# Twelve row gathers a layer move from the value blocks to the key blocks of a PEER layer

## The chip, the cores and the metric

The kernel runs on one core of a Trainium2 chip, which holds five engines that run side by side: TensorE (PE, with its weight loads as PEld), VectorE (DVE), ScalarE (ACT), GpSimd (POOL) and SyncE (SP, which here only issues transfers). The metric is the device time of one execution in microseconds.

## The reference

A trunk of two layers over 512 positions of width 1024. Each layer has a mixer (a spatial gating group and a stick-breaking attention group, which the change does not touch) and a retrieval layer, PEER, which takes most of the time. Cut to PEER:

```python
def peer_ffn(h, wq, k1, k2, u_tab, v_tab):      # 8 heads, 128 keys a half, 16384 experts
    ...
        q = (xb @ wq).reshape(PEER_BLOCK, PEER_HEADS, 2, PEER_HALF)
        ...                                     # top 16 of each half, top 16 of their sums
        eid = jnp.take_along_axis(cand_id, top_pos, axis=-1)
        g = jax.nn.softmax(top_s, axis=-1)
        ue = u_tab[eid]
        ve = v_tab[eid]
        act = jax.nn.gelu(jnp.einsum('pd,phkd->phk', xb, ue))
        return jnp.einsum('phk,phkd->pd', g.astype(xb.dtype) * act, ve)
```

So each position picks 8 x 16 = 128 experts; an expert has one key row `u` and one value row `v` of 1024 numbers.

## The kernel before

The 512 positions are four tiles of 128. They are treated in two ways. For three tiles (384 positions) the kernel is dense: it multiplies all 16384 experts, in 128 blocks of 128 experts, and weighs each product by how much the position wants that expert. For the fourth tile it gathers: for each of its 128 choices one indirect transfer brings 128 rows of 4 KB (512 KB) from the table of keys, and later one from the table of values, 256 gathers a layer.

Dense work. A key block (`u_item`, lines 128 to 130 through `mm3`) is 24 matmuls of 384 columns into a PSUM tile `u`, from one 512 KB weight tile `raw`; ACT splits the weights into `hi` (line 114) and DVE into `lo` (line 117), so that three products make one of full precision. ACT then writes gelu of the result to `act` (line 539, or line 536 into `gu`, where DVE multiplies it into `act` in line 537). A value block (`v_item`) is 18 matmuls of 512 columns into six PSUM tiles `acc`, from one 512 KB tile `wide` or `raw`; beside `hi` and `lo` of the weights it needs `hh` (ACT, line 114) and `hl` (DVE, line 117) of that block's `act`. How much each position wants each expert is made by one-hot products: DVE builds one-hots for 16 positions at once (lines 758, 761 and 765), PE multiplies them for 8 positions at a time (`spread`, lines 773 and 774) into a PSUM tile, and `weigh` brings that to `act` (DVE line 788, ACT line 790). In the second half of the keys that tile is the other one of the two `u` tiles, so it must be emptied before the next key block but one uses it.

Gathered work. Each gather is issued by POOL (line 822) into one of three buffers `grow_`. DVE then multiplies the rows: the first 128 with the activations, to 128 dots (line 825); after the last of them gelu and the weights; the other 128 with these weights, summed up in `hrow` (lines 831 and 833). These are called the gather's product below.

Order. In this part the program's order is written out by hand: each engine runs its instructions in the order in which they were written. `PLAN` has four stages: key blocks 32 to 63, value blocks of the first half, key blocks 64 to 127, value blocks 64 to 127. Each line of it has the kind, the blocks, whether one-hot products are made there (48 of them, spread over the stage) and a number of gathers, which are spread evenly over the blocks:

```python
n1 = min(gathers, (i + 1) * gathers // (n - (6 if bs[-1] == last else 0)))
```

`last` is 127, so that both of the last two stages leave the gathers out of their last 6 blocks. The last stage takes what is left of the 256. What a block brings beside its matmuls is written in the middle of it, in this order (`meanwhile`):

```python
fresh = [spread(*hot.pop(0)) for _ in range(steps[i][1])]
while late:
    late.pop(0)()                  # the products of line 537
for part in fresh:
    weigh(*part)
...                                # hh and hl of the next value block; one-hots
due = min(steps[i][2], len(left))
if due:
    gather(left.pop(0))
prepare(i + LOOK)                  # weights of the block after next: hi and lo
for _ in range(due - 1):
    gather(left.pop(0))
```

So the first gather of a block stands ahead of `lo` for the block after next on DVE, and a second gather behind it. A block with two gathers is called doubled.

Of the kernel before, what the change touches and what calls it, by code (L numbers as in the profile page):

```python
# [31 lines left out]
NK = 128  # L32
# [5 lines left out]
CH = NK // 2  # L38
NS2 = 11
NS1 = CH - NS2  # L40
# [18 lines left out]
FIRST = 2 * UNIT  # L59
HEAD = 1  # L60
MID = 2
PLAN = [("u", range(FIRST, CH), 1, 2),
        ("v", [*range(NS1, CH), *range(NS1)], 0, 100),
        ("u", range(CH, NK), 1, 64),
        ("v", range(CH, NK), 0, 2 * P)]


# [1 line left out]
def trunk(ctx: ExitStack, tc: tile.TileContext, x, rows1, rows2, ada, w_qk, w_row, w_o, wq, kt, wst,  # L69
# [423 lines left out]
    def peer(l):  # L493
        with tc.tile_pool(name="pe", bufs=1) as pe, \
# [237 lines left out]
            with tc.tile_pool(name="gp", bufs=1) as gp, ExitStack() as psc:  # L732
# [61 lines left out]

                order_v = [*PLAN[1][1], *PLAN[3][1]]

# [86 lines left out]

                first, last = PLAN[1][1][0], PLAN[3][1][-1]
                manual = ExitStack()
                manual.enter_context(tc.manual_schedule())
                final, steps, row = [], [], []
                chunk = -1
                for side, bs, spreads, gathers in PLAN:
                    items = [(u_item if side == "u" else v_item)(b) for b in bs]  # L890
# [91 lines left out]
```

## Time and profile before

| what | before |
|---|---|
| median of 3 runs | 3149.47 us (3141.75 to 3155.02) |
| the profiled execution | 3151.26 us, span 3149.6 us |
| PE busy | 2988.5 us, 95% of the span |
| DVE busy | 2485.8 us, 79% |
| POOL busy | 798.6 us, 25% |
| mean rate of all transfers | 207 GB/s |

Times in the profile count from the start of the span. The profiled execution's own time is 1.8 us above the median of the runs. In layer 0 the four stages begin at 573.79, 733.47, 1010.09 and 1317.87 us, in layer 1 at 2119.60, 2279.28, 2553.93 and 2858.00 us; the 58 gathering blocks of the last stage end at 1576.72 and 3110.07 us.

### The profile page before, as it was taken

What the parts mean: (1) busy time and instruction counts of PE and PEld (TensorE: products, weight loads), DVE (VectorE), ACT (ScalarE), POOL (GpSimd) and SP (SyncE); (2) the same over time, 40 slices, a digit from 0 to 9 for tenths busy, and PEclk for the clock granted to TensorE, in tenths of its full rate; (3) what the DMA queues carried; (4) which work ended last, traced back from release to release, by engine and by line L of the source; (5) the groups of instructions that cost most, each with busy time, mean ns of one, the idle gap of its engine ahead of it and who ended that gap; (6) DMA issues with size and microseconds to landing.
All of it is one profiled execution on the core that took longest, in us unless ns stands there. A gap on an engine that the chain in (4) does not pass through costs nothing. (4 is left out here: it accounts for less than half of the span.)

```text
span 3149.6 us, 47135 instructions
## 1 busy us (share of the span) xinstructions
PE 2988.5 (95%) x17532; PEld 2612.1 (83%) x17532; DVE 2485.8 (79%) x4951; ACT 1167.8 (37%) x2016; POOL 798.6 (25%) x584
## 2 busy tenths in 40 slices
PE   5988999999999999999999999999999999999998
PEld 4777888998777999977778888889987789998776
DVE  7687798797778889777853558969887888997787
ACT  3263333333333433333343633324333334333332
POOL 0000000003545323244500000000055543333452
PEclk8999999999999999999999999999999999999999
DMA  8746233337888666688832032333388876667885
GB/s 301 253 159 208 88 101 113 109 108 257 304 305 283 248 215 238 228 313 302 287 117 94 3 107 90 105 114 114 129 307 307 306 268 235 227 233 271 320 304 202
DMA packets 178840, 651.45 MB, mean 207 GB/s; under 512 B 19850, under 2 KB 20274, under 8 KB 178610
## 3 DMA queue, kind: packets, MB, share of 16 engines
q1 hardware_dynamic: 104018, 378.14, 35.8%
q0 software_dynamic: 73728, 268.47, 22.7%
q8 instruction: 137, 2.24, 0.3%
q10 hardware_dynamic: 864, 1.84, 0.2%
q14 instruction: 93, 0.76, 0.1%
HBM read 642.08 MB, written 6.29 MB: 206 GB/s over the span
## 5 line engine op out<-in xcount | busy, mean ns | idle before, releaser
L128 PE MATMUL u<-hh,hi 128*128 128x384 f32 x1920 | 665.1, 346 | 20.1 <-ACT act L539 17.3
L130 PE MATMUL u<-hh,lo 128*128 128x384 f32 x1920 | 648.2, 338 | 5.5 <-DVE lo L117 5.5
L129 PE MATMUL u<-hl,hi 128*128 128x384 f32 x1920 | 647.2, 337 | 0.0
L130 PE MATMUL acc<-hi,hl 128*128 128x512 f32 x1536 | 607.8, 396 | 32.8 <-DVE hl L117 32.5
L129 PE MATMUL acc<-lo,hh 128*128 128x512 f32 x1536 | 602.8, 392 | 7.0 <-DVE lo L117 6.9
L128 PE MATMUL acc<-hi,hh 128*128 128x512 f32 x1536 | 601.1, 391 | 0.0
L117 DVE TENSOR_TENSOR lo<-raw,hi 128x1024 fp32r<-128x1024 f32 x350 | 426.6, 1221 | 193.3 <-ACT hi L114 192.5
L114 ACT ACTIVATE hi<-raw 128x1024 fp32r<-128x1024 f32 x352 | 372.5, 1059 | 521.4 <-PE b L129 132.1
L114 ACT ACTIVATE hh<-act 128x384 fp32r<-128x384 f32 x256 | 134.4, 525 | 680.6 <-PE acc L129 677.5
L128 PEld LDWEIGHTS u<-hh,hi 128*128 128x128 f32 x1920 | 363.9, 190 | 24.7 <-ACT act L539 18.6
L130 PEld LDWEIGHTS acc<-hi,hl 128*128 128x128 f32 x1536 | 289.5, 188 | 113.3 <-DVE hl L117 54.3
L130 PEld LDWEIGHTS u<-hh,lo 128*128 128x128 f32 x1920 | 363.5, 189 | 6.6 <-DVE lo L117 6.6
L129 PEld LDWEIGHTS u<-hl,hi 128*128 128x128 f32 x1920 | 364.4, 190 | 1.4
L129 PEld LDWEIGHTS acc<-lo,hh 128*128 128x128 f32 x1536 | 289.7, 189 | 75.3 <-DVE lo L117 15.1
L128 PEld LDWEIGHTS acc<-hi,hh 128*128 128x128 f32 x1536 | 289.9, 189 | 57.9
L117 DVE TENSOR_TENSOR lo<-wide,hi 128x1024 fp32r<-128x1024 f32 x232 | 283.0, 1220 | 2.2 <-ACT hi L114 2.2
L114 ACT ACTIVATE hi<-wide 128x1024 fp32r<-128x1024 f32 x232 | 242.7, 1046 | 0.0
L117 DVE TENSOR_TENSOR hl<-act,hh 128x384 fp32r<-128x384 f32 (+1 forms) x272 | 152.8, 562 | 17.6 <-ACT hh L114 16.3
L128 PE MATMUL b<-hh,hi 128*128 128x512 f32 x336 | 132.5, 395 | 21.0 <-DVE hh L116 21.0
L234 DVE SCALAR_TENSOR_TENSOR aw<-aw,crow 128x1024 f32<-128x1024 f32 x96 | 116.9, 1222 | 44.9 <-DMA aw<-in_ada 44.6
L536 ACT ACTIVATE gu<-u 128x384 f32<-128x384 f32 (+23 forms) x186 | 63.7, 343 | 199.0 <-PE u L130 199.0
L129 PE MATMUL b<-hl,hi 128*128 128x512 f32 x336 | 131.1, 392 | 0.5 <-DVE hl L117 0.5
(1519 smaller groups left out, 5071.2 us busy)
## 6 DMA issues: line engine op xcount, KB each, us to landing
raw<-in_ut SPq DMA_DIRECT2D x240, 512.0 KB, 3.5
wide<-in_v_rows SPq DMA_DIRECT2D x232, 512.0 KB, 5.0
aw<-in_ada SPq DMA_DIRECT2D x96, 512.0 KB, 4.3
raw<-in_wq SPq DMA_DIRECT2D x32, 512.0 KB, 3.4
raw<-in_w_row SPq DMA_DIRECT2D x24, 512.0 KB, 4.2
raw<-in_v_rows SPq DMA_DIRECT2D x24, 512.0 KB, 6.0
raw<-in_w_qk SPq DMA_DIRECT2D x16, 512.0 KB, 3.5
raw<-in_w_o SPq DMA_DIRECT2D x16, 512.0 KB, 4.0
```

The source lines that it names most:

```text
L114: A.activation(dst_hi, src, AF.Copy)
L117: sub.tensor_tensor(dst_lo, src, dst_hi.bitcast(F32), OP.subtract)
L128: T.matmul(o, lh, rh, start=first, stop=False)
L129: T.matmul(o, lh, rl, start=False, stop=False)
L130: T.matmul(o, ll, rh, start=False, stop=last)
L234: V.scalar_tensor_tensor(aw, aw, 1.0, crow[0], op0=OP.mult, op1=OP.mult, accum_out=modc[:, l, j:j + 1])
L536: A.activation(g[:, :n], pu[:, :n], AF.Gelu_apprx_tanh)
```

## The change

The numbers of gathers in `PLAN` change. The first key stage gets 4 in place of 2, the first value stage 94 for 100, the second key stage 74 for 64, and the last value stage the rest, 84 for 90. In both layers.

```diff
-PLAN = [("u", range(FIRST, CH), 1, 2),
-        ("v", [*range(NS1, CH), *range(NS1)], 0, 100),
-        ("u", range(CH, NK), 1, 64),
+PLAN = [("u", range(FIRST, CH), 1, 4),
+        ("v", [*range(NS1, CH), *range(NS1)], 0, 94),
+        ("u", range(CH, NK), 1, 74),
         ("v", range(CH, NK), 0, 2 * P)]
```

With it the doubled blocks of the second key stage, counted from 0, go from 9, 19, 28, 38, 48 and 57 to 3, 7, 10, 14, 18, 21, 25, 28, 32, 36, 39, 43, 47, 50, 54 and 57; the blocks 3, 10, 18, 25, 28, 43 and 50 also build one-hots (before, 28, 38 and 48). The doubled blocks of the value stages become fewer: 94 gathers over 64 blocks for 100, and 84 over 58 for 90.

In a value stage this is what DVE finds in its order. Before, from block 7 of the first value stage of layer 0 on (`lo` is for weights, `hl` for the next block's `act`, the rows of line 825 are gathers' products):

```order
L825 SCALAR_TENSOR_TENSOR grow__7176,dots<-grow__7176,hrow 128x1024
L117 TENSOR_TENSOR lo<-wide,hi 128x1024
L825 SCALAR_TENSOR_TENSOR grow__7185,dots<-grow__7185,hrow 128x1024
L117 TENSOR_TENSOR hl<-act_2506,hh 128x3x128
L825 SCALAR_TENSOR_TENSOR grow__7208,dots<-grow__7208,hrow 128x1024
L117 TENSOR_TENSOR lo<-wide,hi 128x1024
L825 SCALAR_TENSOR_TENSOR grow__7217,dots<-grow__7217,hrow 128x1024
L117 TENSOR_TENSOR hl<-act_2506,hh 128x3x128
```

And with the change, from the same block on:

```order
L825 SCALAR_TENSOR_TENSOR grow__7182,dots<-grow__7182,hrow 128x1024
L117 TENSOR_TENSOR lo<-wide,hi 128x1024
L117 TENSOR_TENSOR hl<-act_2506,hh 128x3x128
L825 SCALAR_TENSOR_TENSOR grow__7211,dots<-grow__7211,hrow 128x1024
L117 TENSOR_TENSOR lo<-wide,hi 128x1024
L825 SCALAR_TENSOR_TENSOR grow__7220,dots<-grow__7220,hrow 128x1024
L117 TENSOR_TENSOR hl<-act_2506,hh 128x3x128
```

Block 7 has lost its second product, which stood ahead of the next block's `hl`; block 8 is as it was.

In the second key stage the same table adds products to DVE. Before, block 43 of layer 0 (one-hots, one product, `lo`, then the updates of `act` of block 44):

```order
L758 TENSOR_TENSOR wide<-iot,i2t 128x2048
L761 TENSOR_TENSOR om<-iot,i1t 128x1024
L765 TENSOR_TENSOR wide<-om,gt 128x1024 x2
L833 SCALAR_TENSOR_TENSOR hrow<-grow__11386,gg,hrow 128x1024
L117 TENSOR_TENSOR lo<-raw,hi 128x1024
L537 TENSOR_TENSOR act<-act,gu 128x272
L788 SCALAR_TENSOR_TENSOR act_2506<-u_11423,act_2506 128x11x8
L788 SCALAR_TENSOR_TENSOR act<-u_11423,act 128x33x8
```

And with the change:

```order
L758 TENSOR_TENSOR wide<-iot,i2t 128x2048
L761 TENSOR_TENSOR om<-iot,i1t 128x1024
L765 TENSOR_TENSOR wide<-om,gt 128x1024 x2
L833 SCALAR_TENSOR_TENSOR hrow<-grow__11395,gg,hrow 128x1024
L117 TENSOR_TENSOR lo<-raw,hi 128x1024
L833 SCALAR_TENSOR_TENSOR hrow<-grow__11404,gg,hrow 128x1024
L537 TENSOR_TENSOR act<-act,gu 128x272
L788 SCALAR_TENSOR_TENSOR act_2506<-u_11435,act_2506 128x11x8
L788 SCALAR_TENSOR_TENSOR act<-u_11435,act 128x33x8
```

A second product has come between `lo` and the updates that empty the PSUM tile of block 44's one-hot products.

## Rows read from the trace of the kernel before

**Rows 1.** The page's first part: busy time, share of the span and number of instructions of each engine.

```profile
PE 2988.5 (95%) x17532; PEld 2612.1 (83%) x17532; DVE 2485.8 (79%) x4951; ACT 1167.8 (37%) x2016; POOL 798.6 (25%) x584
```

**Rows 2.** Busy time by stretch: start and end of the stretch, its length, then busy time and number of instructions of PE, PEld, DVE, ACT and POOL, the granted share of TensorE's clock, the busy share of the DMA engines and GB/s. In order: layer 0's first key stage, the first 16 and the other 48 blocks of its first value stage, its second key stage, the 58 gathering blocks of its second value stage; layer 1's first value stage in the same two parts.

```profile
573.79:733.47 159.68, 159.68 (x1537) 155.29 (x1537) 143.30 (x221) 63.45 (x174) 5.39 (x4) 1.00 0.37 123
733.47:798.79 65.32, 65.32 (x289) 54.10 (x289) 52.00 (x76) 24.07 (x34) 33.66 (x23) 1.00 0.85 297
798.79:1010.09 211.30, 202.12 (x866) 160.91 (x865) 166.50 (x247) 69.88 (x95) 107.64 (x76) 1.00 0.85 301
1010.09:1317.87 307.78, 298.67 (x2305) 289.04 (x2304) 266.18 (x408) 116.52 (x244) 98.42 (x68) 0.99 0.64 231
1317.87:1576.72 258.85, 244.80 (x1046) 196.03 (x1045) 202.97 (x205) 86.07 (x118) 126.47 (x87) 0.99 0.84 297
2279.28:2344.60 65.32, 65.32 (x289) 54.10 (x289) 52.97 (x78) 24.05 (x34) 34.72 (x24) 1.00 0.86 303
2344.60:2553.93 209.33, 200.72 (x865) 161.06 (x864) 167.36 (x246) 69.61 (x94) 106.73 (x75) 1.00 0.86 303
```

**Rows 3.** PE's waits in the other 48 blocks of layer 0's first value stage (798.79 to 1010.09): who waited for whom, us in total, times, longest.

```profile
PE acc L130 <- DVE hl L117: 6.6, 9, 1.2
PE acc L129 <- DVE lo L117: 2.4, 5, 0.7
```

**Rows 4.** Single instructions in the second value stage of layer 0, in order of time: start, length, engine, line, operation, what it writes and reads; in brackets the engine's idle time before it and what ended it.

```profile
1531.10 1.28 DVE L833 SCALAR_TENSOR_TENSOR hrow<-grow__13927,gg,hrow 128x1024 f32<-128x1024 f32 x1 [0.89 <-DMA grow__13927<-in_v_rows,ids]
...
1532.65 1.68 POOL L822 DMA_INDIRECT grow__13968<-in_v_rows,ids  x1 [2.10 <-DVE hrow L833]
...
1536.68 1.22 DVE L117 TENSOR_TENSOR lo<-wide,hi 128x1024 fp32r<-128x1024 f32 x1
...
1540.96 1.28 DVE L833 SCALAR_TENSOR_TENSOR hrow<-grow__13968,gg,hrow 128x1024 f32<-128x1024 f32 x1 [3.06 <-DMA grow__13968<-in_v_rows,ids]
...
1542.77 0.50 PE L130 MATMUL acc<-hi,hl 128*128 128x512 f32 x1 [3.11 <-DVE hl L117]
```

**Rows 5.** Busy time by stretch, as in rows 2, ahead of that wait's end and after it.

```profile
1538.00:1542.00 4.00, 1.65 (x8) 1.03 (x6) 1.04 (x1) 1.47 (x2) 0.71 (x1) 1.00 0.92 324
1542.00:1547.00 5.00, 4.23 (x12) 3.33 (x13) 5.00 (x7) 0.00 (x0) 2.71 (x3) 0.66 0.57 162
```

**Rows 6.** Six gathers issued one after the other in the same stage; the last number is the time from issue to landing in us.

```profile
grow__13837<-in_v_rows,ids POOLq DMA_INDIRECT x1, 5.6
grow__13866<-in_v_rows,ids POOLq DMA_INDIRECT x1, 6.5
grow__13875<-in_v_rows,ids POOLq DMA_INDIRECT x1, 5.4
grow__13898<-in_v_rows,ids POOLq DMA_INDIRECT x1, 7.9
grow__13927<-in_v_rows,ids POOLq DMA_INDIRECT x1, 7.9
grow__13936<-in_v_rows,ids POOLq DMA_INDIRECT x1, 6.9
```

**Rows 7.** Busy time by stretch of line 833 alone, the gathers' products in the second value stages of layers 0 and 1: the stretch and its length, busy time and number on DVE, granted clock, DMA share, GB/s.

```profile
1317.87:1576.72 258.85, 113.46 (x89) 0.99 0.84 297
2858.00:3110.07 252.07, 112.99 (x89) 0.99 0.85 304
```

**Rows 8.** Single instructions at blocks 48 and 49 of layer 0's second key stage, as in rows 4.

```profile
1248.17 1.28 DVE L833 SCALAR_TENSOR_TENSOR hrow<-grow__11670,gg,hrow 128x1024 f32<-128x1024 f32 x1
...
1250.51 1.28 DVE L833 SCALAR_TENSOR_TENSOR hrow<-grow__11679,gg,hrow 128x1024 f32<-128x1024 f32 x1
...
1252.09 0.62 DVE L788 SCALAR_TENSOR_TENSOR act<-u,act 128x88 f32<-128x88 f32 x2
...
1252.80 0.27 ACT L790 ACTIVATE act<-u 128x120 f32<-128x120 f32 x1 [4.42 <-DVE act L788]
...
1253.13 0.44 PE L128 MATMUL u<-hh,hi 128*128 128x384 f32 x1 [0.64 <-ACT act L790]
```

**Rows 9.** PE's waits in layer 0's second key stage (1010.09 to 1317.87), as in rows 3.

```profile
PE u L773 <- ACT act L539: 4.2, 4, 2.2
PE u L130 <- DVE lo L117: 3.4, 2, 2.0
PE u L128 <- ACT act L790: 1.3, 3, 0.6
```

**Rows 10.** Busy time by stretch, as in rows 2, for groups of five blocks of layer 0's second key stage: blocks 16 to 20, and then every group from 26 to 30 up to 51 to 55.

```profile
1088.85:1111.99 23.14, 23.14 (x185) 22.51 (x185) 20.32 (x38) 9.53 (x19) 7.85 (x6) 1.00 0.61 226
...
1139.07:1163.04 23.97, 23.69 (x186) 22.67 (x185) 21.78 (x32) 9.03 (x19) 7.84 (x6) 1.00 0.61 219
1163.04:1186.19 23.15, 23.15 (x186) 22.52 (x186) 21.39 (x33) 9.13 (x19) 6.90 (x5) 1.00 0.68 241
1186.19:1210.29 24.10, 23.57 (x185) 22.56 (x185) 22.44 (x32) 8.88 (x19) 8.89 (x6) 1.00 0.64 230
1210.29:1233.92 23.63, 23.32 (x185) 22.62 (x185) 21.92 (x32) 8.73 (x19) 8.21 (x5) 1.00 0.63 228
1233.92:1258.22 24.30, 23.60 (x185) 22.57 (x185) 23.11 (x33) 8.61 (x19) 9.82 (x6) 1.00 0.65 232
1258.22:1282.24 24.02, 23.32 (x185) 22.62 (x185) 22.45 (x32) 8.35 (x19) 8.08 (x5) 1.00 0.63 226
```

## The prediction, made before the changed kernel ran

> **What bounds the kernel now.** I read the page's first part, then a table of busy time by stage, then the waits of TensorE in each stage, then single instructions where the longest waits stand. The page says that PE is busy 95% of the span [rows 1], so what a change can win is the time in which PE waits, and the table by stage says where that is [rows 2]. In the first key stage of layer 0 (573.79 to 733.47) PE is busy for all of its 159.68 us. In the first value stage it is busy for all of the first 16 blocks (65.32 us, 4.0825 us a block), and for only 202.12 of the 211.30 us of the other 48. The second key stage loses 9 of 307.78 us and the second value stage 14 of 258.85. (Busy time hides part of a stall, since a matmul's end is modelled; block times show all of it.)
>
> A value block that waits for nothing takes 4.0825 us. So the value stages hold these stalls: first stage, layer 0: 65.32 + 211.30 - 64 x 4.0825 = 15.3 us; layer 1: 65.32 + 209.33 - 261.3 = 13.4 us; second stage, the 58 blocks that gather: 258.85 - 58 x 4.0825 = 22.1 us in layer 0 and, with the time of [rows 7], 252.07 - 236.8 = 15.3 us in layer 1. Together 66 us, the most that the value blocks can give.
>
> Why they wait: PE's waits there all end with DVE's `hl` or `lo` [rows 3], and DVE was late because it stood at a gather's product. The longest case shows the chain [rows 4]: DVE finishes `lo` at 1537.9, its next instruction is the product of grow__13968, whose gather has not landed; DVE idles 3.06 us, does the product at 1540.96, then `hl`, and PE has waited 3.11 us for that `hl`. The clock granted to TensorE is 0.66 of full speed over the next 5 us, where it was 1.00 before [rows 5], so such a wait costs more than itself.
>
> Why the gather is late: it was issued at 1532.65, and POOL had waited for the product of grow__13927 (1531.10 to 1532.38), which frees the buffer; there are three buffers. So gathers run in a circle: product 1.28 us, about 0.27 us to the issue, landing 5.4 to 7.9 us after it, mean 6.7 over six in a row [rows 6]. That is 8.25 us for three gathers, 2.75 each, before any wait behind `lo` and `hl` in DVE's order. The second value stage of layer 0 did 89 products in 258.85 us [rows 7], 2.91 us each, and 89 in 252.07 us in layer 1, 2.83. PE alone would take 4.0825 us x 58 blocks / 90 gathers = 2.63 us a gather: the gathers, not PE, set the pace there. The first 16 blocks are free of stalls since three gathers lie ready and DVE starts ahead.
>
> The DMA rule of the Trainium skill would have it otherwise. Its page "DMA: Bandwidth & Descriptors", section "Anatomy of one DMA — SWDGE (gpsimd) path", gives 2.0 us plus the bytes at 436 GB/s, an estimate of 3.2 us for these 512 KB. By that the circle would be 4.8 us, 1.6 us a gather, far below PE's need, and nothing would be won. The rows say 5.4 to 7.9 us beside the weight stream, so here the trace disagrees, and the rows decide.
>
> **The change, part by part.** Value blocks, 6 gathers fewer in each stage. If gathers set the pace, a stage's time follows their number until PE's own time is reached. First stage: 276.62 x 94/100 = 260.0 us and 274.65 x 0.94 = 258.2 us, both just below PE's 261.3: no stall by the mean (PE's own time per gather rises from 2.61 to 2.78 us). Second: 258.85 x 84/90 = 241.6, 4.8 us above 236.8; 252.07 x 84/90 = 235.3, below it. But landings are uneven, and pace and need are now nearly equal, so single late landings still reach PE. I keep a fifth of today's stall for that: 3.1 and 2.7 us in the first stages, 3.1 us in the second stage of layer 1, and the 4.8 us of layer 0. So 66 us become 13.7, and 52 us are won. The bounds: all 66, if the head start of the first 16 blocks covers the unevenness; a half, 33, if single late landings weigh more than the mean.
>
> First key stage, 2 more gathers (blocks 7 and 23 beside 15 and 31). Each adds one product to DVE, whose busy time is 143.30 of 159.68 us, and PE waits for nothing there [rows 2]; the two gathers that it has today cost PE nothing. Cost 0; if that cover of 16 us were used up, 2 x 1.28 = 2.6 us a layer.
>
> Second key stage, 10 more gathers. Spread over 58 blocks, two products now fall into one block 16 times instead of 6. The circle does not press here: the three buffers serve 1.28 gathers per 4.7 us, 3.7 us each, against the 2.75 to 2.91 that they can do. The price is DVE's time. An extra product stands ahead of the block's `act` updates, which empty the PSUM tile that the next key block needs. The row for one such block late in the stage shows it [rows 8]: two products at 1248.17 and 1250.51, the update at 1252.09, ACT's part at 1252.80 after 4.42 us of idling, and PE waits 0.64 us for that. PE's waits in the stage are of this sort [rows 9], beside two at its start and one at the end of the first 128 gathers, which stay.
>
> To price it I cut the stage into groups of five blocks, which repeat [rows 10]. A group without a stall takes 23.15 us (1163.04). An early group with a doubled block (1088.85) takes 23.14: no cost, DVE has 2.8 us to spare. Three late ones with a doubled block that also builds one-hots take 23.97, 24.10 and 24.30, and the groups behind the last two 23.63 and 24.02. So the three cost 0.82, 0.95 + 0.48 and 1.15 + 0.87: 1.4 us each on average, the dearest 2.0. Of the ten added, about half come in the first 25 blocks; there DVE still has some 2.8 us a group, and I put 0.3 us on each for the denser rhythm. The others meet a DVE that is busy 21.4 to 23.1 of 23.15 us, and I put their own 1.28 us on each, near the mean measured. That is 1.5 + 6.4 = 7.9 us a layer, 16 us in all. The bounds: nothing, as the early pair shows, and 2.0 us for each of ten in both layers, 40 us; I take the value nearest the late rows for the late half alone.
>
> Traffic only moves: DMA's share is 0.64 in this key stage against 0.85 in the value stages, so ten more transfers of 512 KB fit. POOL is busy 98 of 307.78 us. The products change place, not number.
>
> Sum: -52 + 16 = -36 us. The profiled execution took 3151.3 us, so 3115; the median of the three runs is 1.8 us lower, so **3113 us**.
>
> **Rivals.** *The stall stays.* Each of PE's waits follows one late landing, and landings might be as late with fewer gathers, since the weight stream beside them is the same. Then the value blocks give nothing and the key blocks cost 16 us: 3165 us, or 3182 with the dearest price on the late half and 1.28 us on the early one. It ends slower once less than 16 of the 66 us go. Against it: the first 16 blocks have the same weight stream beside them (297 GB/s against 301 [rows 2]) and no stall, and the stage's time is the number of gathers times the circle. Chance 0.05. By the rule of the Trainium skill named above ("DMA: Bandwidth & Descriptors") it would end the same way, since the circle would not bind.
>
> *Half the stall stays*, and the added products cost 20 us as DVE fills up: 3149.5 - 33 + 20 = 3136 us. For it: a single wait of 3.06 us at a mean that is almost in balance. Chance 0.2.
>
> *Bytes set the pace, not the circle.* The value stages move 301 GB/s; 24 gathers of 0.524 MB are 12.6 MB, 42 us at that rate; with the cost 16, 3123 us. Against it: the share of the DMA engines is 0.85, not 1. Chance 0.1.
>
> *All goes well:* the whole 66 us, cost 6 us: 3089 us. For it: the mean pace falls below PE's need in three stages of four. Chance 0.15.
>
> **How the numbers follow.** The forecast has 0.5, for 3100 to 3126. The range of 3095 to 3138 takes in the half-stall case and the bandwidth case, and leaves out the stall that stays and most of the best case, about 0.2 together. A change of 0.5% is 15.7 us, about what runs from 3141.75 to 3155.02 can tell: faster means below 3133.7. Forecast, bandwidth and best case lie there, and 0.08 of the half case: 0.83. Slower than 3165.2 is the stall that stays, 0.05. Within 0.5%: 0.12.
>
> **What would show it.** Right: value blocks at 4.08 us for most of both stages, first stages near 264 us and the 58 blocks near 240; PE's waits for `hl` and `lo` down to a fifth; DVE's idling at gathered rows with them. Second key stages 7 to 8 us longer, with more waits for ACT's `act` and doubled groups near 24.5 us; the first key stage still 159.68 us. Wrong: value stages whose landings lengthen as PE speeds up, or five-block groups over 26 us in the second key stage, which would mean that DVE has no room left.

## The result, and the profile after

The changed kernel takes 3100.57 us (median of 4 runs, 3096.85 to 3102.64); the kernel before took 3149.35 beside it (4 runs, 3141.75 to 3155.02). The ratio is 0.9845, with an interval from 0.9828 to 0.9862: 49 us, 1.5%, faster. The forecast was 3113, in a range of 3095 to 3138. The profiled execution took 3101.2 us, 1.7 us of it outside its span of 3099.5.

The page's first part, after, answers to [rows 1]:

```profile
PE 2973.4 (96%) x17532; PEld 2611.9 (84%) x17532; DVE 2479.3 (80%) x4951; ACT 1166.8 (38%) x2016; POOL 807.0 (26%) x584
```

The counts are the same. PE's busy time is 15 us shorter and the span 50 us: the time came out of waits, a part of which counts as busy, since a matmul's end is modelled. The table by stretch shows which. It answers to [rows 2] and has its columns: start and end, length, busy time and number of instructions of PE, PEld, DVE, ACT and POOL, granted clock, DMA share, GB/s. In order: layer 0's first key stage, the first 16 and the other 48 blocks of its first value stage, its second key stage, the 58 gathering blocks of its second value stage; layer 1's first value stage in the same two parts, and the 58 blocks of its second value stage.

```profile
573.43:733.11 159.68, 159.68 (x1538) 155.28 (x1538) 145.34 (x225) 63.32 (x174) 8.76 (x6) 1.00 0.38 129
733.11:798.43 65.32, 65.32 (x290) 54.09 (x289) 51.64 (x76) 24.07 (x34) 33.51 (x23) 1.00 0.84 298
798.43:998.18 199.75, 198.80 (x865) 161.83 (x864) 160.13 (x236) 70.97 (x95) 102.37 (x70) 1.00 0.85 305
998.18:1304.05 305.87, 299.30 (x2305) 289.03 (x2304) 275.44 (x420) 115.33 (x243) 111.29 (x77) 0.99 0.69 248
1304.05:1544.95 240.90, 238.68 (x1045) 195.60 (x1045) 196.24 (x200) 86.12 (x118) 119.62 (x81) 1.00 0.85 307
2248.02:2313.34 65.32, 65.32 (x289) 54.09 (x289) 51.63 (x77) 24.06 (x34) 33.41 (x23) 1.00 0.82 296
2313.34:2512.62 199.28, 197.19 (x865) 161.85 (x864) 160.85 (x237) 70.73 (x95) 103.06 (x71) 1.00 0.86 307
2816.58:3060.00 243.42, 240.22 (x1046) 195.45 (x1045) 196.38 (x200) 86.12 (x118) 119.22 (x81) 1.00 0.85 303
```

Set against [rows 2] and [rows 7]:

| stage | before, layers 0 and 1 | after | forecast |
|---|---|---|---|
| first key stage | 159.68, 159.68 | 159.68, 159.68 | no change |
| first value stage | 276.62, 274.65 | 265.07, 264.60 | near 264 |
| second key stage | 307.78, 304.07 | 305.87, 303.96 | 7.9 longer |
| second value stage, 58 blocks | 258.85, 252.07 | 240.90, 243.42 | near 240 |

The four value stages gave 11.55 + 10.05 + 17.95 + 8.65 = 48.2 us. The second key stages, which were to cost 16, gave another 1.9 + 0.1: together 50.2 us, where the span lost 50.1.

PE's waits answer to [rows 3] and [rows 9] (us in total, times, longest): the later 48 blocks of layer 0's first value stage, then three rows of its second key stage, then the 58 blocks of its second value stage.

```profile
PE acc L129 <- DVE lo L117: 0.7, 2, 0.4
...
PE u L773 <- ACT act L539: 2.8, 2, 2.2
PE u L130 <- DVE lo L117: 2.4, 2, 2.0
PE u L128 <- ACT act L790: 0.8, 2, 0.6
...
PE acc L130 <- DVE hl L117: 2.1, 2, 1.4
```

Before, the 58 blocks of the second value stage had:

```profile
PE acc L130 <- DVE hl L117: 12.1, 10, 3.1
PE acc L129 <- DVE lo L117: 2.0, 5, 1.0
```

In the first value stage 6.6 and 2.4 us of waiting have become 0.7, in the second 12.1 and 2.0 have become 2.1. In the second key stage every row became shorter, where ten more products should have made them longer. The five-block groups answer to [rows 10]: blocks 16 to 20 of layer 0's second key stage, then every group from 26 to 30 up to 51 to 55.

```profile
1076.77:1100.47 23.70, 23.62 (x186) 22.59 (x186) 21.95 (x41) 9.67 (x20) 7.84 (x6) 1.00 0.71 258
...
1125.94:1149.91 23.97, 23.67 (x186) 22.65 (x186) 22.81 (x33) 9.03 (x19) 11.54 (x7) 1.00 0.69 241
1149.91:1173.05 23.14, 23.14 (x185) 22.51 (x185) 22.48 (x34) 9.13 (x19) 7.84 (x6) 1.00 0.73 263
1173.05:1196.20 23.15, 23.15 (x186) 22.52 (x185) 22.48 (x32) 8.70 (x19) 10.56 (x7) 1.00 0.68 245
1196.20:1220.43 24.23, 23.62 (x186) 22.60 (x186) 23.74 (x34) 8.83 (x20) 9.89 (x6) 1.00 0.70 253
1220.43:1243.87 23.44, 23.38 (x186) 22.55 (x186) 23.05 (x33) 8.60 (x19) 9.83 (x6) 1.00 0.70 252
1243.87:1267.85 23.98, 23.33 (x186) 22.64 (x186) 23.60 (x32) 7.82 (x19) 10.96 (x7) 1.00 0.67 245
```

The group 36 to 40 (1173.05) holds two doubled blocks, 36 and 39, and takes 23.15 us, the time of a group without a stall; before, with the one doubled block 38, it took 24.10. The group 46 to 50 holds 47 and 50 and takes 23.44, for 24.30 with 48 alone. The group 51 to 55 holds 54 and takes 23.98, for 24.02 with none. More products, and in two groups less time: it seems that the price of a product hangs on where it stands. The experiments had to say why, and whether the circle of three buffers is what set the value stages' pace.

### The profile page after: what moved, and what is told of

The parts are those of the page before. It is cut to its first block, busy times and chain, and to the rows that moved or that the text cites. A ratio compares the mean times of both kernels' runs of the same rounds, so it can differ in the third digit from the quotient of the medians.

```text
span 3099.5 us, 47121 instructions
## 1 busy us (share of the span) xinstructions
PE 2973.4 (96%) x17532; PEld 2611.9 (84%) x17532; DVE 2479.3 (80%) x4951; ACT 1166.8 (38%) x2016; POOL 807.0 (26%) x584
## 5 line engine op out<-in xcount | busy, mean ns | idle before, releaser
L130 PE MATMUL u<-hh,lo 128*128 128x384 f32 x1920 | 648.1, 338 | 4.4 <-DVE lo L117 4.4
L130 PE MATMUL acc<-hi,hl 128*128 128x512 f32 x1536 | 601.4, 392 | 4.6 <-DVE hl L117 4.6
L117 DVE TENSOR_TENSOR lo<-raw,hi 128x1024 fp32r<-128x1024 f32 x350 | 426.6, 1221 | 193.0 <-ACT hi L114 192.6
L130 PEld LDWEIGHTS u<-hh,lo 128*128 128x128 f32 x1920 | 363.5, 189 | 5.9 <-DVE lo L117 5.9
L130 PEld LDWEIGHTS acc<-hi,hl 128*128 128x128 f32 x1536 | 288.4, 188 | 71.3 <-DVE hl L117 12.0
L117 DVE TENSOR_TENSOR lo<-wide,hi 128x1024 fp32r<-128x1024 f32 x232 | 283.1, 1220 | 2.1 <-ACT hi L114 2.1
L117 DVE TENSOR_TENSOR hl<-act,hh 128x384 fp32r<-128x384 f32 (+1 forms) x272 | 152.9, 562 | 21.9 <-ACT hh L114 20.7
L130 PE MATMUL b<-hh,lo 128*128 128x512 f32 x336 | 131.2, 391 | 0.0
```

Of the source, the lines that this page charges most:

```text
L117: sub.tensor_tensor(dst_lo, src, dst_hi.bitcast(F32), OP.subtract)
L130: T.matmul(o, ll, rh, start=False, stop=last)
```

## Experiments

Each kernel was timed on one chip with the kernel before, which took 3154.96 us beside the fourth buffer, the two kernels with doubled blocks written out by hand and the one with more gathers in the first key stage; 3156.24 beside two buffers, the change with the fourth buffer and the two plans of the last experiment; and 3148.71 beside the four with every fifth block doubled. Two buffers and these four were executed once.

**A fourth buffer, nothing else.** If gathers run in a circle through three buffers, a fourth must free the value stages under the old plan. To make room, two constant tiles of the mixer move into the mixer's own pool; line 128 is 122 there, while the lines of the PEER part keep their numbers.

```diff
-                    r = gp.tile([P, D], F32, name="grow_", bufs=3)
+                    r = gp.tile([P, D], F32, name="grow_", bufs=4)
```

> The kernel before, with a fourth buffer for gathered rows and nothing moved (two small constant tiles are made in the mixer instead of at the start, to free the room). Theory of the circle: four gathers per circle of 8.25 to 8.73 us are 2.1 to 2.2 us each, below the 2.63 us that PE needs per gather, so the value stages fall close to PE's own time (first stages 261 to 266 us, the 58 blocks 237 to 243 us) with all their gathers in place, and the whole takes 3083 to 3100 us. Rival, bytes or DVE's time set the pace: both are unchanged, the value stages stay at 275 and 252 to 259 us, and the whole stays within 6 us of 3149 us.

Measured: 3078.42 us (3076.42 to 3082.09), ratio 0.9764, interval 0.9738 to 0.9789. Layer 0's first value stage, second key stage and second value stage by stretch, columns as above:

```profile
732.52:993.68 261.16, 261.16 (x1154) 216.22 (x1153) 223.29 (x328) 95.20 (x128) 145.63 (x99) 1.00 0.91 323
993.68:1294.70 301.02, 296.33 (x2306) 287.40 (x2305) 262.06 (x402) 115.84 (x243) 96.17 (x66) 1.00 0.65 232
1294.70:1531.38 236.68, 236.68 (x1046) 195.94 (x1045) 206.23 (x207) 86.31 (x118) 126.48 (x86) 1.00 0.90 324
```

PE is busy for the whole of both value stages: 261.16 and 236.68 us are its own time, with all 100 and 90 gathers in them. The 66 us of the prediction's first part are all there, without moving a gather; the whole is even below the band of 3083 to 3100, by what the key stages gave. And the rival of the bytes falls: 323 GB/s where it held 301 for the limit. Landings did not become shorter. Three gathers in a row of the second value stage (the last number is us from issue to landing):

```profile
grow__13744<-in_v_rows,ids POOLq DMA_INDIRECT x1, 5.9
grow__13753<-in_v_rows,ids POOLq DMA_INDIRECT x1, 8.0
grow__13776<-in_v_rows,ids POOLq DMA_INDIRECT x1, 6.9
```

The mean over the stage's 86 is 7.3 us, where 87 of the kernel before averaged 6.8. A circle of 1.28 + 0.27 + 7.3 = 8.85 us through four buffers is 2.21 a gather, well under PE's 2.63.

The second key stages have become 6.8 and 1.7 us shorter too, with no change to their plan. PE's waits in layer 0's:

```profile
PE u L773 <- ACT act L539: 3.2, 3, 2.2
PE u L122 <- ACT act L790: 1.3, 3, 0.6
```

The row `PE u L130 <- DVE lo L117` of [rows 9] (3.4 us, at the stage's start) has no counterpart: DVE no longer arrives late from the value stage. Blocks 1 to 5 took 27.14 and 25.82 us before, and take 23.15 in both layers here. So 4.0 and 2.7 us that I had seen in the key stages belonged to the value stages' circle. Blocks 21 to 25 are 1.6 us shorter in layer 0 and 1.6 longer in layer 1, which is the clock of the last section.

**Two buffers.** The other side of the same theory.

```diff
-                    r = gp.tile([P, D], F32, name="grow_", bufs=3)
+                    r = gp.tile([P, D], F32, name="grow_", bufs=2)
```

> The kernel before with two buffers for gathered rows in place of three, nothing moved. Theory of the circle: a gather takes half a circle. With landings as before, 8.25 to 8.73 us over two are 4.1 to 4.4 us each, so 100 gathers make the first value stages 410 to 440 us long and 90 make the second ones 370 to 395 us. If landings shorten with the lighter traffic to the 5.6 us of the shortest rows, a circle is 7.2 us, and the stages are 360 and 325 us. Rival, bytes or DVE's time set the pace: 275 and 255 us as before.

Measured, one execution: 3462.18 us. Layer 0's first and second value stage, then three landings of the second:

```profile
735.66:1084.89 349.23, 289.27 (x1153) 219.25 (x1153) 219.58 (x321) 94.16 (x128) 140.89 (x98) 0.97 0.69 238
...
1404.99:1722.27 317.28, 261.24 (x1046) 197.75 (x1045) 202.04 (x202) 85.87 (x118) 125.12 (x87) 0.97 0.70 240
...
grow__13651<-in_v_rows,ids POOLq DMA_INDIRECT x1, 4.4
grow__13660<-in_v_rows,ids POOLq DMA_INDIRECT x1, 5.7
grow__13683<-in_v_rows,ids POOLq DMA_INDIRECT x1, 6.1
```

The first stage takes 3.49 us a gather, the second 3.53. The mean landing is 5.5 us, so the circle is 7.0 us, 3.5 for each of two buffers. Pace is circle over buffers in both directions; but the landing is no constant. In the second value stage it averages 5.5, 6.8 and 7.3 us with two, three and four buffers, so that both stages are a little shorter than the 360 and 325 us expected of shorter landings.

**The change with the fourth buffer.** Without late landings the price of the added products stands alone. The plan is the change's, 4/94/74/84 (gathers in the four stages), and the two constant tiles are moved as in every kernel with four buffers. Against the change:

```diff
-                    r = gp.tile([P, D], F32, name="grow_", bufs=3)
+                    r = gp.tile([P, D], F32, name="grow_", bufs=4)
```

> The changed kernel with four buffers. The value stages stand at PE's own time (261.2 and 236.7 us) with either plan, so that what is left between this kernel and the one before with four buffers is the price of the added products in the key stages alone. If that price is what the prediction said, 16 us, this kernel takes 3094 us against 3078. If the late groups of the changed kernel are the measure (3.0 to 3.5 us of stall a layer against 4.3 to 4.6 before), the two agree within 4 us.

Measured: 3081.59 us (3080.02 to 3083.21), ratio 0.9762, interval 0.9734 to 0.9789. The second key stages of both layers:

```profile
996.62:1300.63 304.01, 299.10 (x2305) 289.15 (x2304) 273.34 (x417) 115.45 (x243) 108.75 (x76) 0.99 0.69 247
2501.58:2804.70 303.12, 298.83 (x2306) 289.28 (x2305) 271.97 (x416) 115.38 (x243) 108.69 (x76) 0.99 0.69 248
```

Against 301.02 and 302.38 with four buffers and the old plan, the twelve moved gathers cost 3.0 and 0.7 us here (the medians differ by 3.2, on two chips whose kernel before differs by 1.3), and gain nothing, since nothing is left to gain in the value stages. In layer 0, 1.6 of the 3.0 us come from blocks 21 to 25 alone, of which the last section tells.

**Which block is doubled.** Two kernels keep the change's plan and three buffers, and write out by hand which 16 blocks of the second key stage take two gathers: all on blocks that build one-hots, or none.

```diff
+TWICE = (10, 13, 15, 18, 20, 25, 28, 30, 33, 38, 40, 43, 45, 48, 50, 53)
...
+                        if side == "u" and bs[-1] == last:
+                            n1 = min(gathers, min(i + 1, n - 6) + sum(d <= i for d in TWICE))
```

> The changed kernel with the same numbers of gathers, but all 16 doubled blocks of the second key stage put on blocks that also build one-hots. Theory that the price hangs on the kind of block: ten late ones at about 1 us and six early ones at 0.3 us are 12 us a layer against some 4 us in the changed kernel, so the stage takes 311 to 316 us, and the whole 3113 to 3121 us. Theory that it hangs on the number of added products alone: the stage stays at 304 to 306 us and the whole at 3101 us.

In the other kernel `TWICE` is (6, 9, 12, 16, 19, 22, 26, 29, 31, 34, 36, 41, 44, 46, 51, 56).

> The changed kernel with the same numbers of gathers, but all 16 doubled blocks of the second key stage put on blocks that build no one-hots. Theory of the kind of block: the late groups fall to 23.15 us, the stage loses 3 to 4 us a layer (300 to 302 us), and the whole takes 3092 to 3096 us. Theory of the number alone: 304 to 306 us and 3101 us as in the changed kernel.

Measured, on one-hots: 3114.19 us (3101.02 to 3116.86), ratio 0.986, interval 0.9826 to 0.9894; second key stages 309.00 and 308.12. Off one-hots: 3106.91 (3106.16 to 3116.27), ratio 0.9859, interval 0.9829 to 0.9889; 304.51 and 305.44. Blocks 36 to 40 and 46 to 50 of layer 0, on one-hots:

```profile
1176.67:1200.80 24.13, 23.59 (x185) 22.57 (x185) 22.69 (x33) 8.88 (x19) 8.90 (x6) 1.00 0.67 241
...
1225.40:1250.06 24.66, 23.74 (x186) 22.65 (x186) 24.34 (x34) 8.61 (x19) 10.95 (x7) 1.00 0.73 261
```

and off them:

```profile
1174.41:1198.63 24.22, 23.95 (x185) 22.71 (x185) 23.58 (x35) 9.07 (x20) 9.63 (x6) 1.00 0.73 259
...
1221.81:1246.50 24.69, 24.28 (x185) 22.71 (x185) 24.21 (x35) 8.83 (x20) 9.56 (x6) 1.00 0.72 255
```

The first went as its price for a late double said (blocks 26 to 55 hold 8.6 and 10.0 us over 23.15 a group in the two layers), though below the band for the stage. The whole does not tell it from the change: the intervals of the two ratios overlap. The second missed: 4.1 and 4.6 us where almost nothing was expected, and its stages are as long as the theory of the number alone had said (304 to 306 us). Here doubled blocks stood two apart (34 and 36, 44 and 46) and right behind one-hot blocks, so either closeness, or the place behind, or simply DVE's filling up could be meant. The next four runs separate the last two from the place.

**Every fifth block.** One-hots are built on the blocks whose number ends in 0, 3, 5 or 8, a rhythm of five blocks. With four buffers, 4/94/69/89 gathers and the doubled blocks exactly five apart, only the place in that rhythm differs between four kernels. Against the change with four buffers, doubled from 3:

```diff
-        ("u", range(CH, NK), 1, 74),
+        ("u", range(CH, NK), 1, 69),
...
+TWICE = (3, 8, 13, 18, 23, 28, 33, 38, 43, 48, 53)
```

> Four buffers, 4/94/69/89 gathers, doubled blocks of the second key stage 3, 8, ... 53: each also builds one-hots, and the next block has updates of act. All value stages at PE's own time (261.2 and 236.7 us). Theory 'place' (a second product costs where it lengthens the stretch between a one-hot build and the next block's updates): the six late ones cost about 0.9 us each, so the groups 26 to 55 hold 4 to 6.5 us over 23.15 in each layer, where the kernel without a doubled key block held 0.1. Theory 'full DVE' (any second product costs, wherever it stands): also 4 to 6.5 us. Theory 'behind' (it costs right behind a one-hot block): under 1.5 us.

> As the run from 3, with the doubled blocks 4, 9, ... 54: right behind a block that builds one-hots, none built in it. Theory 'place': the stretch to the next updates is short, the groups 26 to 55 hold under 1 us over 23.15 in a layer. 'Full DVE': 4 to 6.5 us. 'Behind': 3 to 5 us.

> As the run from 3, with the doubled blocks 1, 6, ... 51: right behind a block that builds one-hots, and the one block of five without one-hot products (4.16 us instead of 4.75). 'Place': under 1 us over 23.15 in the groups 26 to 55 of a layer, since it has no updates and the lag is made up in the next block. 'Full DVE': 4 to 6.5 us. 'Behind': 3 to 5 us.

> As the run from 3, with the doubled blocks 2, 7, ... 52: neither on nor right behind a block that builds one-hots. 'Place' and 'behind': under 1 us over 23.15 in the groups 26 to 55 of a layer. 'Full DVE': 4 to 6.5 us.

Measured, each once: 3090.47, 3074.62, 3065.33 and 3068.56 us. Over 23.15 us a group, blocks 26 to 55 hold 7.3 and 8.3 us (layers 0 and 1) from 3, above the band; 1.1 and 0.8 from 4; 0.8 and 0.7 from 1; 0.8 and 0.7 from 2. Single executions can tell that much, since the same groups repeat in both layers. Blocks 41 to 45 of layer 0, first doubled from 3:

```profile
1192.17:1216.86 24.69, 23.73 (x185) 22.65 (x185) 23.00 (x33) 8.73 (x19) 9.14 (x6) 1.00 0.65 235
```

then from 4, from 1 and from 2:

```profile
1189.38:1212.60 23.22, 23.22 (x186) 22.59 (x185) 22.73 (x32) 8.51 (x20) 9.88 (x6) 1.00 0.68 250
```

```profile
1186.73:1209.87 23.14, 23.14 (x185) 22.51 (x185) 22.68 (x33) 8.63 (x19) 9.91 (x6) 1.00 0.70 252
```

```profile
1186.19:1209.34 23.15, 23.15 (x185) 22.52 (x185) 22.69 (x33) 8.63 (x19) 9.88 (x6) 1.00 0.70 250
```

The third busy time of each row is what to read: DVE has 23.00, 22.73, 22.68 and 22.69 us of work, the same within a few tenths, and the first group takes 1.5 us longer. In blocks 26 to 30 the run from 3 has even less DVE work than the run from 2, 21.47 us for 21.73, and loses 0.8 us where that one loses 0.1. So it isn't DVE's load ("full DVE" falls for these blocks), nor the place right behind a one-hot block ("behind" falls: 4 and 1 stand there). It is the stretch from a one-hot build to the next block's updates of `act`, for whose end ACT and then PE wait. These updates empty the tile that the very next key block needs, not "the next key block but one", as the description of the kernel has it: in [rows 8] the update at 1252.09 is block 49's, and the matmul at 1253.13 that waits for it is block 50's first. By the program's order only the blocks ending in 3 and 8 build one-hots and are followed by a block with such updates; those ending in 1 and 6 have none.

Two things stay beside the place. The price grows along the stage: from 3, blocks 6 to 10 of layer 0 lose 0.3 us and blocks 51 to 55 2.0. And in blocks 51 to 55, where DVE has 23.3 to 23.4 us of work for a stretch of 23.15, the runs from 4, 1 and 2 lose 0.5 to 0.7 us too, most of what they lose at all; there a full DVE does cost.

PE's waits over blocks 26 to 55 of layer 0 in the run from 3 (lines 128, 790, 773 and 539 are 125, 793, 776 and 542 there):

```profile
PE u L125 <- ACT act L793: 3.0, 6, 0.7
PE u L776 <- ACT act L542: 1.0, 2, 0.6
```

Six waits for that update, one per late double. The run from 2 has no row in the same blocks. That a second product on a block ending in 0 or 5 costs alone was not tried; in the run on one-hots such blocks stood among the others. For the run off one-hots closeness is left. Its trace reads that way: with 44 and 46 doubled, the update of block 47 starts 4.5 us after the block, and the block takes 5.58 us; in the run from 1, with 46 doubled and not 44, it is 3.2 us and 4.75. No run tries closeness alone, and these two also differ in their buffers, so this is not shown.

**More gathers in the first key stage.** The prediction bounded their cost by a cover of 16 us; 14 gathers there, 10 of them taken from the second key stage again, use it up. Against the kernel before (the second key stage keeps its 64):

```diff
-PLAN = [("u", range(FIRST, CH), 1, 2),
-        ("v", [*range(NS1, CH), *range(NS1)], 0, 100),
+PLAN = [("u", range(FIRST, CH), 1, 14),
+        ("v", [*range(NS1, CH), *range(NS1)], 0, 94),
```

> Twelve gathers a layer leave the value blocks as in the change, but all go to the first key stage (14 in place of 2), and the second key stage keeps its 64. The value stages should be as with the change (265 and 241 to 243 us), the second key stage as before (304 to 308 us). If the first key stage has DVE time to cover them, as its 16 idle us say, it stays at 159.7 us and the whole takes about 3102 us. If it has not, 12 products of 1.28 us add up to 15 us a layer, and the whole takes up to 3132 us.

Measured: 3117.80 us (3113.04 to 3118.32), ratio 0.988, interval 0.9854 to 0.9906. Layer 0's first key stage and PE's waits in it:

```profile
573.98:738.90 164.92, 161.44 (x1537) 155.35 (x1537) 155.70 (x245) 61.90 (x174) 26.07 (x16) 1.00 0.45 157
...
PE u L130 <- DVE lo L117: 1.6, 4, 0.6
PE g L773 <- DVE wide L765: 1.0, 2, 0.8
```

Twelve more products cost 5.2 us a layer: DVE has 155.70 us of work in what was 159.68, and is late with `lo` and with one-hots. That is between the two cases expected. The value stages took 264 to 268 and 239 to 246 us, the second key stages 305.8, as expected. Two more products, the change's own, cost nothing.

**Back to the value blocks.** If a fourth buffer makes gathers free in value blocks, the best plan goes the other way from the change. With four buffers, against the change:

```diff
-        ("v", [*range(NS1, CH), *range(NS1)], 0, 94),
-        ("u", range(CH, NK), 1, 74),
+        ("v", [*range(NS1, CH), *range(NS1)], 0, 104),
+        ("u", range(CH, NK), 1, 52),
```

With 4 gathers in the first key stage, 96 are left for the last stage.

> Four buffers, and the gathers moved the other way: 4, 104, 52 and 96, so that no block of the second key stage is doubled and six of its blocks have none. The circle of four allows 2.2 us a gather against the 2.47 that PE leaves. DVE has 1.22 + 0.55 us for a value block's lo and hl and 1.66 products of 1.3 us, 3.9 of 4.08 us. If that still fits, the value stages stay at 261.2 and 236.7 us, the second key stage loses its 4 to 5 us of late waits a layer, and the whole takes 3066 to 3074 us. If DVE sets the pace there, stalls come back in the value stages and it takes 3080 us or more.

Between the two stands 4/100/58/94, also with four buffers: one gather in each gathering block of the second key stage, none doubled.

> Four buffers with 4, 100, 58 and 94 gathers: each of the 58 blocks of the second key stage has exactly one. The value stages keep the load of the kernel before and should stay at 261.2 and 236.7 us, the late waits of the key stage go with the doubled blocks (4 to 5 us a layer), and the whole takes 3067 to 3073 us. If late waits do not hang on doubled blocks, it takes 3078 us as with the plan of before.

Measured: 3063.85 us (3062.70 to 3064.76) for the first, ratio 0.9705, interval 0.9678 to 0.9732; 3070.04 (3069.14 to 3071.68) for the second, ratio 0.9725, interval 0.9698 to 0.9752. The first is below its band, the second within. The first is 92 us faster than the kernel before on its chip, and its ratio lies clear of the change's 0.9845. Layer 0's first value stage, second key stage and second value stage, and layer 1's second key stage:

```profile
733.40:994.56 261.16, 261.16 (x1154) 216.22 (x1153) 224.66 (x332) 94.87 (x128) 148.36 (x103) 1.00 0.92 328
994.56:1290.93 296.37, 295.13 (x2305) 286.94 (x2304) 251.74 (x388) 116.42 (x244) 84.85 (x55) 1.00 0.61 217
1290.93:1527.61 236.68, 236.68 (x1045) 195.95 (x1045) 212.30 (x213) 86.38 (x118) 130.91 (x92) 1.00 0.92 338
2492.20:2786.66 294.46, 294.46 (x2305) 286.91 (x2304) 249.06 (x384) 115.77 (x243) 83.96 (x54) 1.00 0.61 217
```

104 and 96 gathers fit into value stages that still take PE's own time, and layer 1's second key stage has no stall left: its 294.46 us are all PE busy. The 6 us by which the second is slower are not the price of its six more gathers in key blocks: without a doubled block it holds 0.1 us over 23.15 a group in blocks 26 to 55 of layer 0 and none in layer 1, and loses 3.9 us in blocks 21 to 25 of each layer, of which the last section tells.

## Why the prediction was right, and where a term was not

**What bounds it: right.** PE waited in the value stages for DVE, DVE for a gather, the gather for one of three buffers. Four buffers took the whole wait away and two made the pace 3.5 us a gather.

**The time follows the number of gathers down to PE's own time: right, a little too hopeful.** I kept 13.7 us of stall and 17.8 were left: 3.8 and 3.3 us in the first stages, 4.1 in the second stage of layer 0 and 6.6 in that of layer 1, where 3.1 stood. The rest scatters: the two kernels that place 16 doubles by hand have the same first value stages, and theirs took 265.7 to 270.0 us for the change's 265.07 and 264.60.

**First key stage at nothing: right**, 159.68 us again. The cover is less wide than 16 us, though: twelve products of 1.28 us, 15.4 in all, cost 5.2 of them.

**Second key stage at 16 us: wrong, and the step is the price of the late half.** I put 0.3 us on each of five early products and 1.28 on each of five late ones, 1.5 + 6.4 a layer, "near the mean measured". With the circle out of the way the early term holds: blocks 1 to 20 grew by 1.7 us in layer 0 and 0.9 in layer 1 between the two four-buffer kernels. The late term does not: blocks 26 to 63 changed by -0.3 and -0.1 us, not +6.4. In the change itself blocks 1 to 20 grew by 0.4 and 0.6 us and blocks 26 to 63 shrank by 0.7 in each layer; blocks 21 to 25 of layer 0 shrank by 1.6, by the clock. The three late rows from which I priced, blocks 28, 38 and 48 [rows 10], were all at the one dear place in the rhythm of five, and I read their price as that of any late product. The new plan keeps two late doubles at that place, 28 and 43, drops 38 and 48, and puts 32, 36, 39 and 47 where they cost little; 50, which builds one-hots, and 54, which falls where DVE is full, cost some (23.44 and 23.98 us for their groups). The rows to see this by were there: [rows 8] shows the wait as one of the update behind a one-hot block, and the list of doubled blocks with one-hots stands in the description of the change.

Another misreading had no weight here. The 3.4 us of waiting for `lo` at the stage's start [rows 9], which I took for the key stage's own, came from the value stage before it, since it went with the fourth buffer. In the change it shrank only to 2.4, and behind it the granted clock fell to its lower level of 1.2 GHz for a part of the group (0.94 over the whole), so that blocks 1 to 5 of layer 0 did not become shorter. Before, then after:

```profile
1014.27:1041.41 27.14, 23.71 (x185) 22.45 (x185) 24.16 (x39) 10.03 (x21) 10.26 (x7) 1.00 0.73 265
...
1002.37:1030.29 27.92, 25.43 (x185) 24.04 (x185) 24.28 (x39) 10.07 (x22) 12.61 (x8) 0.94 0.68 240
```

**The number: in part luck.** The gain of the value stages was put 4 us too high and the cost of the key stages 18 us too high. One error took off a part of the other, and the range reached 18 us below the forecast.

**The rivals.** The stall that stays and half the stall: 48 of 66 us went, neither. Bytes: refuted by 323 GB/s and more with four buffers. All goes well: in total a little nearer (3089) than the forecast, but neither of its terms held, since 17.8 us of stall were left and the key stage cost nothing. The Trainium skill's page "DMA: Bandwidth & Descriptors", section "Anatomy of one DMA — SWDGE (gpsimd) path", gives the estimate of 3.2 us a gather that the prediction weighed. These runs disagree with it further: with two buffers and a DMA share of 0.70 the shortest of 87 gathers took 4.1 us and the mean was 5.5.

## What to carry to other kernels

Where a ring of buffers sets the pace, its number is circle time over buffers against the consumer's need, and one more buffer may be worth more than moving the work: here 2.4% against 1.5%, after which the better plan moved gathers the opposite way (3.0%). Before pricing an added instruction by rows of its kind, check whether those rows share a place in a rhythm; a busy share near 100% of an in-order engine says less than which result it delays. And a wait at a stage's start can belong to the stage before.

## What had not been expected of the hardware

Landing time is not a property of the transfer alone. The same 512 KB gathers took 5.5 us on average with two buffers (240 GB/s, DMA share 0.70, second value stage of layer 0), 6.8 with three (297 GB/s, 0.84 [rows 2]) and 7.3 with four (324 GB/s, 0.90): with more in flight each was slower, and all together faster. The number of buffers alone does not do it: in the second key stages of layer 0, where the DMA share is 0.62 to 0.65, the means are 5.7, 5.9 and 5.7 us with two, three and four.

The same wait of TensorE can cost nearly twice as much. In blocks 21 to 25 of layer 0's second key stage PE waits 2.2 us for `act` (line 539), which on ACT stands behind the gelu of the 128 dots (line 828), before and after. By stretch, before:

```profile
1111.99:1139.07 27.08, 24.89 (x185) 24.19 (x185) 20.95 (x38) 9.63 (x20) 6.16 (x5) 0.94 0.62 217
```

and after:

```profile
1100.47:1125.94 25.47, 23.28 (x186) 22.59 (x185) 21.45 (x40) 9.58 (x20) 7.85 (x6) 1.00 0.72 247
```

After the change the granted clock stayed at its upper level of 2.4 GHz (1.00) through the wait; before it, it fell to its lower level of 1.2 GHz for a part of the group (0.94 over the whole), and PE's busy time is 1.6 us longer. Over the 23.15 us of a group without a stall, the wait cost 3.9 us in one case and 2.3 in the other. In blocks 1 to 5 it is the other way round: both kernels have a wait of 2.0 us there, and the clock fell in the changed one. What decides it, no run shows; layer 1 of the kernel before took 25.50 us. In both kernels the 128th gather stands in block 23, which builds one-hots. One block earlier the group takes 23.15 us (back to the value blocks); one later it takes 23.57 (doubled from 1), but 25.39 where it is that block's second gather (doubled from 4).
